# Low parts of weights later in VectorE's queue, two convolution blocks later, taps earlier

## The chip, the cores and the metric

The kernel runs on one core of one Trainium2 chip. The metric is device microseconds (us) of one execution, from launch to end; lower is better. A profiled execution also has a span, from its first to its last instruction.

## The reference

The reference is an encoder trunk of two layers with width 1024, applied with the same weights to a sequence of 256 tokens and to one of 512. It is all in float32. Per layer:

```
h  = rms_norm(x)                       # 768 tokens x 1024
q (8 heads), k, v (2 heads each), u (2 x 1024), gl (2 x 1024) = h @ w_in
q, k: rms_norm per head, rotary positions;  a = softmax(q k^T / sqrt(128)) v
c  = silu(layer_norm(conv31(u_a * sigmoid(u_g)))) @ w_pw     # depthwise, 31 taps
x += (sigmoid(gl_a) * a + sigmoid(gl_c) * c) @ w_out
x += (silu(gate) * up) @ w_down,  gate, up = rms_norm(x) @ w_gu   # 2816 wide
```

A last rms_norm follows the second layer. The change concerns what lies between `h` and `w_pw`: the projections, the attention and the convolution.

## The kernel before

**Layout and precision.** Activations lie with features on the 128 partitions and the 768 tokens along the free axis; a convolution chunk is 128 channels wide and there are 8 of them (j = 0 to 7). Each float32 operand is split into a high part (rounded by ScalarE) and a low part (the difference, by VectorE or GpSimd), and a product takes three matmuls: high by high, low by high, high by low. A weight block of 128 x 1024 arrives by DMA in a stage buffer (`Stage.load`, SP's queue); `Unit.make` has ScalarE write the high part and one other engine the low part. For all units of size 2 but those of `w_out` that engine is VectorE (`Weights.engines`, line 345). Stage buffers, high and low parts share a ring of 12 (N_W); at most four stage buffers are loaded ahead (`staged`, N_WS), and `Weights.pump` loads and splits the next block as soon as the counts let it.

**One program written by a planner.** The engines run their queues in program order, and the program order is written by a planner, `Clock`. Its `now` is advanced by each matmul at columns / 2400 us (`mm`, line 203), and its `dve` account by each VectorE instruction at elements / 960 us and a constant (`Vector`, line 133): 0.13 us, and TAP_MORE for a conv tap of 783 elements. A job given to `clock.at` or `clock.later` is written into the program once `now` has passed its due time, or before that when something calls it.

**The stream.** A layer's projections are blocks in the order of the list FILL: `ag2` (conv chunks 0 and 1, two weight blocks each), `k`, `q:0` to `q:3`, `v`, `gl:0` to `gl:15` (gates), `ag:2` to `ag:7` (a conv chunk each). The first seven run alone. Then attention begins: 48 units (8 heads x 6 query tiles) of scores, softmax, transposes and, for every two tiles, values; between their parts `fill` runs stream blocks for FILL_US planned us a unit. When FILL is done, the fill turns to the blocks of `w_pw` at the pace LATE_US.

**Softmax of a unit.** VectorE takes the row maximum (line 133, tile `h3t0st` for head 3, tile 0), ScalarE the exponential, GpSimd the reciprocal of the sum (line 1332), ScalarE scales, TensorE transposes (line 207), ScalarE and VectorE split the transposed tile.

**The convolution.** `ag_half` (line 795) takes a buffer for z, the gated input, out of three (N_Z). While three are live it issues taps, line 797: `while y.z_live >= N_Z: clock.tap()`. GpSimd then clears the padding of the new buffer (memset, line 803). A conv chunk is a first step on ScalarE and 30 taps on VectorE, each y += z shifted x weight (128 x 783). Two chunks are in progress at a time (`Clock.chains`) and their taps alternate. `Clock.tick` issues taps as long as `dve` is less than TAP_AHEAD = 1 us ahead of `now`. When all 8 chunks are summed, `channel_norm` runs LN_AFTER = 5.2 planned us later: means, centring, squares, variance, scaling, silu. The first pointwise block forces whatever of this has not been issued (`clock.force(y)`, line 895).

Of the kernel before, what the change touches and what calls it, by code (L numbers as in the profile page):

```python
# [118 lines left out]
class Vector:  # L119
# [5 lines left out]
    def __getattr__(self, name):  # L125
        f = getattr(self.engine, name)

        def call(out, *args, **kw):
            n = 1
            for d in (args[0].shape if name == "tensor_reduce" else out.shape)[1:]:  # L130
                n *= d
            self.clock.vector(n / 960.0 + (TAP_MORE if n == CONV_N else 0.13))
            return f(out, *args, **kw)  # L133
# [22 lines left out]
def trunk(tc, x_in, x_tok, w_a, w_qkv, w_pw, w_out, w_gu, w_down, vecs, gqk, rope, y_out):  # L156
    nc = tc.nc
    clock = Clock()
    vector = Vector(nc.vector, clock)

    with ExitStack() as ctx:
# [48 lines left out]
        def act(out, in_, func=AF.Copy, **kw):  # L210
            nc.scalar.activation(out, in_, func, **kw)  # L211

        def sub_lo(engine, lo, x, hi):
            engine.tensor_tensor(lo, x, hi.bitcast(F32), op=ALU.subtract)  # L214
# [6 lines left out]
        class Stage:  # L221


            def __init__(self, name, src):
                self.name, self.src, self.tile, self.last = name, src, None, None
# [5 lines left out]
        class Unit:  # L231
# [2 lines left out]

            def __init__(self, name, stages):
                self.name, self.stages, self.out, self.live = name, stages, None, False
                for stage in stages:
                    stage.last = self

            def make(self, engines):  # L240
                hi = wpool.tile([P, 1024], F32R, name="hi_" + self.name, tag="w", bufs=N_W)
                lo = wpool.tile([P, 1024], F32R, name="lo_" + self.name, tag="w", bufs=N_W)
                stage = self.stages[0].tile
                act(hi, stage)
                n = 1024 // len(engines)
                for i, e in enumerate(engines):
                    sl = slice(i * n, (i + 1) * n)
                    sub_lo(e, lo[:, sl], stage[:, sl], hi[:, sl])
                self.out = (hi, lo)

        class Quarter(Unit):

# [6 lines left out]
            def make(self, engines):  # L259
                src = self.quad.operand(self.m)  # L260
                both = wpool.tile([P, 1024], F32R, name="wq_" + self.name, tag="w", bufs=N_W)
                hi, lo = both[:, :512], both[:, 512:]
                act(hi, src)
                sub_lo(engines[0], lo, src, hi)
                self.out = (hi, lo)

        class Quad:

# [19 lines left out]
        class Weights:  # L288
# [36 lines left out]
            def split(self, engines=(nc.gpsimd,)):  # L325
                w = self.all[self.ready]
                while not self.here(w):
                    assert self.load()
                assert self.live + w.size + max(self.staged, N_WS) <= N_W
                self.live += w.size  # L330
                w.live = True
                w.make(engines)
                self.staged -= sum(stage.last is w for stage in w.stages)
                self.ready += 1
                self.next = max(self.next, clock.now + W_STEP[w.size - 1])

            def pump(self):
                while self.load():
                    pass
                if self.ready < len(self.all) and clock.now >= self.next:  # L340
                    w = self.all[self.ready]
                    if self.here(w) and self.live + w.size + max(self.staged, N_WS) <= N_W:
                        self.split(self.engines(w))
# [5 lines left out]
            def get(self, w):  # L349
                while w.out is None:  # L350
                    self.split(self.engines(self.all[self.ready]))
                return w.out

            def free(self, w):
# [60 lines left out]
        weights = Weights()  # L415
# [217 lines left out]
        def layer_blocks(l):  # L633
# [127 lines left out]
            def conv(j, z):  # L761
                wcol = lambda k: vcol(l, V_WDW, k * KC + j)

                def first():
                    y.y[j] = UC(nm(f"y{j}"))
                    act(y.y[j], z[:, :CONV_N], AF.Identity, scale=wcol(0), bias=vcol(l, V_BDW, j))
# [23 lines left out]
                def ready():  # L790
                    first()
                    clock.at(FIRST_AT[1], lambda: clock.waiting.append(taps))
                clock.at(FIRST_AT[0], ready)

# [45 lines left out]
            def gl_body(idx):  # L840
                def body(ws):
# [3 lines left out]
                    for s, (t0, n) in enumerate(SPLITS):  # L845
                        pg = yield from proj_a(ws[0], y.hT, s, nm(f"gl{idx}_{s}"))
                        act(sg[:, t0:t0 + n], pg[:, :n])
                        if s == 0 and FILL[-1] == f"gl:{idx}":
                            y.h_free = 1
# [9 lines left out]

            for b in FILL:  # L860
                kind, _, n = b.partition(":")
# [435 lines left out]
        def attention(y):  # L1297
# [7 lines left out]
            def scores(n):  # L1305
# [22 lines left out]

                late = stream.done((l, FILL[-1]))
                jobs[n] = [  # L1330
# [55 lines left out]
            def fill():  # L1386
                goal[0] += FILL_US / 2
                if not stream.done((l, FILL[-1])):
                    stream.run(goal[0], (l, FILL[-1]))
                    if stream.done((l, FILL[-1])):  # L1390
                        goal[0] = stream.work
                        goal[0] += PW_START
                        y.late = clock.now + 8.0
                        y.h_free = 2
                        split_z(y)
                elif y.m_done:
                    goal[0] = max(goal[0] + (LATE_US - FILL_US) / 2, stream.work)
                    stream.run(goal[0], (l, f"pw:{min(y.m_done, PW_MAX) - 1}"))
# [21 lines left out]
        def channel_norm(y):  # L1420
# [59 lines left out]
            def scale(j):  # L1480
                def f():
                    for s, (t0, n) in enumerate(SPLITS):
                        sl = slice(YO[s], YO[s] + n)
                        vector.tensor_tensor(ys[j][:, sl], ys[j][:, sl], rstd[s][:, :n], op=ALU.mult)
                    if j in SILU_AT:
                        clock.at(0.5, lambda: silus(j))
                return f

            def silus(j1):
                split_z(y)  # L1490
                for j in range(y.silus, j1 + 1):
                    act(ys[j], ys[j], AF.Silu, scale=vcol(l, V_LNG, j), bias=vcol(l, V_LNB, j))
                    y.silus += 1
                    split_z(y)
                if y.silus == KC:
                    y.normed()
# [116 lines left out]
        clock.drain()  # L1613


FILL = ["ag2", "k", "q:0", "gl:0", "ag:4", "ag:2", "ag:3", "gl:8", "v", "gl:9", "gl:1", "q:1", "ag:5", "ag:6",
        "gl:10", "gl:2", "q:2", "ag:7", "gl:3", "gl:14", "gl:12", "gl:4", "gl:11", "q:3", "gl:5", "gl:13", "gl:7",
        "gl:15", "gl:6"]
SILU_AT = (5, 7)
FIRST_AT = (1.2, 1.4)  # L1620
BURSTS = ((1, 7), (6, 4), (5, 2), (3,))
D_FIRST = (4.0, 6.0)
# [11 lines left out]
BEFORE = 7  # L1634
SIG_MAX = 3
SIG_LEFT = 25
FILL_US = 6.3
LATE_US = 3.7
PW_MAX = 10
PW_START = 3.0  # L1640
# [6 lines left out]
RSTD_AFTER = 5.4  # L1647
TABLES_AT = 16.0
TAP_AHEAD = 1.0
TAP_MORE = 0.13  # L1650
W_STEP = (0.9, 2.9)
A_EXP = 2.2
A_REC = (3.5, 2.5)
# [91 lines left out]
```

## Time and profile before

| | us |
|---|---|
| median of 3 runs | 2441.3 (2438.95 to 2444.44) |
| the profiled execution's own time | 2443.3 |
| its span | 2441.5 |
| TensorE busy in it | 2226.4 |
| VectorE busy in it | 1876.5 |

A row of a wait names the waiting engine, the tile and line it works on, and the instruction that released it. All operations of VectorE have line 133, most matmuls line 203, transposes line 207, and activations line 211, since helpers record them; so tiles are told by name: `L_y` a convolution's sum, `L_z` its input, `L_h3t0p` the probabilities of head 3, tile 0, `lo_L_wgl` the low part of a gate weight. In names `L0_` and `L1_` are both `L_`. Layer 0 runs from the start to about 1210 us, layer 1 after it; the same instruction appears some 1210 us later.

### The profile page before, as it was taken

How to read it: one execution, taken by the hardware profiler on the slowest of the kernel's cores; microseconds unless marked ns; L12 is line 12 of the kernel's file. 1: busy time of each engine (PE TensorE's matmuls, PEld its weight loads, DVE VectorE, ACT ScalarE, POOL GpSimd, SP SyncE). 2: the span in 40 equal slices, each digit the busy share in tenths (PEclk: the TensorE clock that was granted, in tenths of full speed). 3: DMA queues.
4: the chain of work that ended last, by engine and by line, in shares of the span. 5: the costliest groups of instructions: out<-in, count | busy, mean ns of one | idle time of the engine just before them, and what ended most of it. 6: DMA issues, size and time to landing. Idle time of an engine off the chain costs nothing. (4 is left out here: it accounts for less than half of the span.)

```text
span 2441.5 us, 34896 instructions
## 1 busy us (share of the span) xinstructions
PE 2226.4 (91%) x13276; PEld 2095.6 (86%) x13276; DVE 1876.5 (77%) x2484; ACT 1143.8 (47%) x2289; POOL 1068.2 (44%) x935
## 2 busy tenths in 40 slices
PE   8999869949979999999989998698699799999997
PEld 7989859848979999999988898596589799999997
DVE  5899768956387788798968897689553877987888
ACT  5446536555244444444443555465642444444443
POOL 3704132311256666666445142131112666666663
PEclk9999989969989999999999999899799899999998
DMA  4112111213312343343421111112142133333332
GB/s 165 61 57 69 66 39 63 77 43 113 133 49 90 121 144 116 124 145 113 152 85 61 63 63 57 50 63 72 54 146 101 35 121 127 124 130 137 122 123 87
DMA packets 72423, 229.59 MB, mean 94 GB/s; under 512 B 8128, under 2 KB 15296, under 8 KB 72256
## 3 DMA queue, kind: packets, MB, share of 16 engines
q1 hardware_dynamic: 72256, 227.37, 27.1%
q8 instruction: 104, 1.70, 0.3%
q14 instruction: 63, 0.52, 0.1%
HBM read 208.46 MB, written 18.87 MB: 93 GB/s over the span
## 5 line engine op out<-in xcount | busy, mean ns | idle before, releaser
L133 DVE SCALAR_TENSOR_TENSOR L_y<-L_z,vec,L_y 128x783 f32<-128x783 f32 x480 | 496.1, 1077 | 0.8
L214 POOL TENSOR_TENSOR wq_L_wgu_0m<-T_L_wgu,wq_L_wgu_0m 128x512 fp32r<-128x512 f32 x168 | 228.6, 1376 | 173.8 <-ACT wq_L_wgu_0m L211 173.8
L211 ACT ACTIVATE wq_L_wgu_0m<-T_L_wgu 128x512 fp32r<-128x512 f32 x168 | 102.7, 630 | 259.3 <-DVE T_L_wgu L133 208.7
L214 POOL TENSOR_TENSOR wq_L_wgu_0m<-st_L_wgu,wq_L_wgu_0m 128x512 fp32r<-128x512 f32 x126 | 179.3, 1425 | 43.4 <-ACT wq_L_wgu_0m L211 42.7
L203 PE MATMUL L_gl<-L_h1h,hi_L_wgl 128*128 128x512 f32 (+1 forms) x512 | 176.6, 345 | 0.0
L203 PE MATMUL L_gl<-L_h1h,lo_L_wgl 128*128 128x512 f32 (+1 forms) x512 | 173.2, 338 | 0.0
L203 PE MATMUL L_gl<-L_h1l,hi_L_wgl 128*128 128x512 f32 (+1 forms) x512 | 172.9, 338 | 0.0
L203 PEld LDWEIGHTS L_gl<-L_h1h,lo_L_wgl 128*128 128x128 f32 x512 | 97.0, 189 | 11.0
L203 PEld LDWEIGHTS L_gl<-L_h1l,hi_L_wgl 128*128 128x128 f32 x512 | 97.2, 190 | 9.2
L203 PEld LDWEIGHTS L_gl<-L_h1h,hi_L_wgl 128*128 128x128 f32 x512 | 97.0, 190 | 9.1
L203 PE MATMUL L_c<-L_zsl,hi_L_wpw 128*128 128x256 f32 (+1 forms) x256 | 89.2, 348 | 9.5 <-DVE L_zsl L133 9.5
L203 PE MATMUL L_c<-L_zsh,hi_L_wpw 128*128 128x256 f32 (+1 forms) x256 | 92.1, 360 | 4.6 <-ACT L_zsh L211 4.6
L203 PE MATMUL L_ug<-L_h1h,lo_L_wu 128*128 128x256 f32 (+1 forms) x256 | 89.0, 348 | 2.8 <-DVE lo_L_wu L133 2.8
L133 DVE TENSOR_TENSOR L_dl<-L_silu,L_dh 128x384 fp32r<-128x384 f32 x80 | 59.5, 783 | 41.0 <-ACT L_dh L211 41.0
L203 PE MATMUL L_ug<-L_h1h,hi_L_wu 128*128 128x256 f32 (+1 forms) x256 | 90.6, 354 | 0.0
L203 PE MATMUL L_ua<-L_h1h,lo_L_wu 128*128 128x256 f32 (+1 forms) x256 | 88.6, 346 | 1.4 <-DVE lo_L_wu L133 1.4
L203 PE MATMUL L_ua<-L_h1h,hi_L_wu 128*128 128x256 f32 (+1 forms) x256 | 89.7, 350 | 0.0
L203 PE MATMUL L_ug<-L_h1l,hi_L_wu 128*128 128x256 f32 (+1 forms) x256 | 89.5, 349 | 0.0
L211 ACT ACTIVATE wq_L_wgu_0m<-st_L_wgu 128x512 fp32r<-128x512 f32 x126 | 78.5, 623 | 22.8 <-POOL wq_L_wgu_0m L214 19.8
L203 PE MATMUL L_c<-L_zsh,lo_L_wpw 128*128 128x256 f32 (+1 forms) x256 | 88.9, 347 | 0.0
L203 PE MATMUL L_ua<-L_h1l,hi_L_wu 128*128 128x256 f32 (+1 forms) x256 | 88.1, 344 | 0.0
L203 PE MATMUL L_o<-L_mTlo,hi_L_wo 128*128 128x384 f32 x256 | 86.4, 338 | 0.0
(1630 smaller groups left out, 7626.7 us busy)
## 6 DMA issues: line engine op xcount, KB each, us to landing
st_L_wgu<-w_gu SPq DMA_DIRECT2D x88, 512.0 KB, 3.5
st_L_wu<-w_a SPq DMA_DIRECT2D x32, 512.0 KB, 3.5
st_L_wgl<-w_a SPq DMA_DIRECT2D x32, 512.0 KB, 3.5
st_L_wqkv<-w_qkv SPq DMA_DIRECT2D x24, 512.0 KB, 3.5
st_L_wpw<-w_pw SPq DMA_DIRECT2D x16, 512.0 KB, 3.5
st_L_wo<-w_out SPq DMA_DIRECT2D x16, 512.0 KB, 3.6
g_dram<-L_sgl SPq DMA_DIRECT2D x16, 384.0 KB, 3.0
L_gj<-g_dram SPq DMA_DIRECT2D x16, 384.0 KB, 3.8
```

What stands on the lines that cost most here:

```text
L133: return f(out, *args, **kw)
L203: nc.tensor.matmul(out, lhsT, rhs, start=start, stop=stop)
L211: nc.scalar.activation(out, in_, func, **kw)
L214: engine.tensor_tensor(lo, x, hi.bitcast(F32), op=ALU.subtract)
```

## The change

VectorE's low part of a weight block is no longer issued right after the high part but as a job due 1.6 planned us later (LO_AFTER), or when the block is first asked for by a matmul (`Weights.get`). The stage buffer counts as used once the low part is issued (`Weights.used`). In FILL, `ag:6` changes places with `gl:10`, and `ag:7` moves behind `gl:3` and `gl:14`. FILL_US goes from 6.3 to 6.5, and TAP_MORE from 0.13 to 0.02, so the planner books 0.11 us less for each conv tap. Instructions and their number stay the same.

```diff
--- before.py
+++ after.py
@@ -234,6 +234,7 @@
 
             def __init__(self, name, stages):
                 self.name, self.stages, self.out, self.live = name, stages, None, False
+                self.low = lambda: None
                 for stage in stages:
                     stage.last = self
 
@@ -243,10 +244,18 @@
                 stage = self.stages[0].tile
                 act(hi, stage)
                 n = 1024 // len(engines)
-                for i, e in enumerate(engines):
-                    sl = slice(i * n, (i + 1) * n)
-                    sub_lo(e, lo[:, sl], stage[:, sl], hi[:, sl])
+
+                def low():
+                    for i, e in enumerate(engines):
+                        sl = slice(i * n, (i + 1) * n)
+                        sub_lo(e, lo[:, sl], stage[:, sl], hi[:, sl])
+                    weights.used(self)
+
                 self.out = (hi, lo)
+                if engines == (vector,):
+                    self.low = clock.later(LO_AFTER, low)
+                else:
+                    low()
 
         class Quarter(Unit):
 
@@ -263,6 +272,7 @@
                 act(hi, src)
                 sub_lo(engines[0], lo, src, hi)
                 self.out = (hi, lo)
+                weights.used(self)
 
         class Quad:
 
@@ -330,9 +340,11 @@
                 self.live += w.size
                 w.live = True
                 w.make(engines)
-                self.staged -= sum(stage.last is w for stage in w.stages)
                 self.ready += 1
                 self.next = max(self.next, clock.now + W_STEP[w.size - 1])
+
+            def used(self, w):
+                self.staged -= sum(stage.last is w for stage in w.stages)
 
             def pump(self):
                 while self.load():
@@ -349,6 +361,7 @@
             def get(self, w):
                 while w.out is None:
                     self.split(self.engines(self.all[self.ready]))
+                w.low()
                 return w.out
 
             def free(self, w):
@@ -1613,10 +1626,11 @@
         clock.drain()
 
 
-FILL = ["ag2", "k", "q:0", "gl:0", "ag:4", "ag:2", "ag:3", "gl:8", "v", "gl:9", "gl:1", "q:1", "ag:5", "ag:6",
-        "gl:10", "gl:2", "q:2", "ag:7", "gl:3", "gl:14", "gl:12", "gl:4", "gl:11", "q:3", "gl:5", "gl:13", "gl:7",
+FILL = ["ag2", "k", "q:0", "gl:0", "ag:4", "ag:2", "ag:3", "gl:8", "v", "gl:9", "gl:1", "q:1", "ag:5",
+        "gl:10", "ag:6", "gl:2", "q:2", "gl:3", "gl:14", "ag:7", "gl:12", "gl:4", "gl:11", "q:3", "gl:5", "gl:13", "gl:7",
         "gl:15", "gl:6"]
 SILU_AT = (5, 7)
+LO_AFTER = 1.6
 FIRST_AT = (1.2, 1.4)
 BURSTS = ((1, 7), (6, 4), (5, 2), (3,))
 D_FIRST = (4.0, 6.0)
@@ -1634,7 +1648,7 @@
 BEFORE = 7
 SIG_MAX = 3
 SIG_LEFT = 25
-FILL_US = 6.3
+FILL_US = 6.5
 LATE_US = 3.7
 PW_MAX = 10
 PW_START = 3.0
@@ -1647,7 +1661,7 @@
 RSTD_AFTER = 5.4
 TABLES_AT = 16.0
 TAP_AHEAD = 1.0
-TAP_MORE = 0.13
+TAP_MORE = 0.02
 W_STEP = (0.9, 2.9)
 A_EXP = 2.2
 A_REC = (3.5, 2.5)
```

## Rows read from the trace of the kernel before

**Rows 1.** Page: span, and busy time of each engine.

```profile
span 2441.5 us, 34896 instructions
PE 2226.4 (91%) x13276; PEld 2095.6 (86%) x13276; DVE 1876.5 (77%) x2484; ACT 1143.8 (47%) x2289; POOL 1068.2 (44%) x935
```

**Rows 2.** Waits of TensorE: waiter, releaser: us in total, times, longest.

```profile
PE L_h3t0T L207 <- ACT L_h3t0p L211: 42.6, 2, 21.3
PE L_var L203 <- DVE L_sq L133: 40.3, 2, 20.1
...
PE L_h1t5T L207 <- ACT L_h1t5p L211: 13.0, 2, 6.5
...
PE L_rstd L207 <- DVE L_rb L133: 5.2, 2, 2.6
PE L_c L203 <- ACT L_zsh L211: 4.6, 2, 2.3
```

**Rows 3.** Timeline of VectorE: start, us, instruction, count.

```profile
247.66 8.59 DVE L133 SCALAR_TENSOR_TENSOR L_y<-L_z,vec,L_y 128x783 f32<-128x783 f32 x9
...
324.03 15.20 DVE L133 SCALAR_TENSOR_TENSOR L_y<-L_z,vec,L_y 128x783 f32<-128x783 f32 x16
```

**Rows 4.** Timeline of GpSimd; in brackets idle time before and its releaser.

```profile
256.31 0.20 POOL L803 MEMSET L_z<- 128x15 f32 x3 [12.74 <-DVE L_y L133]
...
339.29 0.20 POOL L803 MEMSET L_z<- 128x15 f32 x3 [19.29 <-DVE L_y L133]
...
344.59 0.54 POOL L1332 TENSOR_TENSOR L_h3t0st<-L_h3t0st,nones 128x1 f32<-128x1 f32 x1
```

**Rows 5.** Windows: length, busy PE, PEld, DVE, ACT, POOL, clock, DMA.

```profile
339.50:376.00 36.50, 30.28 (x164) 26.24 (x165) 15.90 (x24) 20.00 (x38) 7.01 (x9) 0.86 0.25 83
376.00:483.40 107.40, 107.40 (x692) 97.04 (x691) 97.74 (x120) 62.44 (x134) 33.85 (x33) 1.00 0.21 72
240.00:483.40 243.40, 215.58 (x1372) 194.20 (x1371) 194.60 (x241) 130.20 (x274) 62.42 (x71) 0.94 0.18 61
1450.00:1693.40 243.40, 215.57 (x1367) 194.30 (x1367) 193.49 (x240) 130.44 (x275) 62.39 (x71) 0.94 0.18 61
```

**Rows 6.** Timeline of VectorE and TensorE at the end of the convolution.

```profile
483.41 0.96 DVE L133 TENSOR_TENSOR L_ysum<-L_ysum,L_y 128x783 f32<-128x783 f32 x1
484.43 1.56 PE L203 MATMUL L_mean<-L_ysum,ones 128*128 128x256 f32 x4 [0.18 <-DVE L_ysum L133]
...
515.24 0.58 PE L203 MATMUL L_c<-L_zsh,hi_L_wpw 128*128 128x256 f32 x1 [2.30 <-ACT L_zsh L211]
```

**Rows 7.** Timeline of TensorE: first score matmuls, three units apart.

```profile
402.66 0.39 PE L203 MATMUL L_h4t2s<-L_kThi,L_q2Thi 128*128 128x512 f32 x1
...
429.44 0.39 PE L203 MATMUL L_h4t5s<-L_kThi,L_q2Thi 128*128 128x512 f32 x1
```

**Rows 8.** Window of instructions on L_z: length, DVE, ACT, POOL, clock, DMA.

```profile
376.00:483.40 107.40, 66.73 (x66) 1.03 (x1) 0.00 (x0) 1.00 0.21 72
```

**Rows 9.** Group of VectorE, 50 to 240 us: busy, mean ns, idle before.

```profile
L133 DVE SCALAR_TENSOR_TENSOR L_y<-L_z,vec,L_y 128x783 f32<-128x783 f32 x114 | 119.9, 1095 | 0.2
```

**Rows 10.** Windows after the two waits, columns as in rows 5.

```profile
264.30:268.00 3.70, 3.70 (x11) 3.12 (x12) 1.12 (x3) 2.43 (x6) 0.54 (x1) 0.51 0.11 35
345.60:350.00 4.40, 4.28 (x12) 3.48 (x13) 2.16 (x3) 3.17 (x9) 0.10 (x1) 0.52 0.20 62
```

**Rows 11.** Groups of VectorE, 240 to 484 us, columns as in rows 9.

```profile
L133 DVE SCALAR_TENSOR_TENSOR L_y<-L_z,vec,L_y 128x783 f32<-128x783 f32 x125 | 127.1, 1059 | 0.2
L133 DVE TENSOR_TENSOR lo_L_wgl<-st_L_wgl,hi_L_wgl 128x1024 fp32r<-128x1024 f32 x12 | 15.4, 1281 | 19.1 <-ACT hi_L_wgl L211 19.1
L133 DVE TENSOR_TENSOR lo_L_wqkv<-st_L_wqkv,hi_L_wqkv 128x1024 fp32r<-128x1024 f32 x4 | 4.9, 1223 | 4.1 <-ACT hi_L_wqkv L211 4.1
```

**Rows 12.** Timeline of TensorE: the wait for a weight's low part.

```profile
101.71 0.39 PE L203 MATMUL L_ua<-L_h1h,lo_L_wu 128*128 128x256 f32 x1 [0.57 <-DVE lo_L_wu L133]
```

**Rows 13.** Timeline of GpSimd: a reciprocal beside taps.

```profile
281.52 1.31 POOL L1332 TENSOR_TENSOR L_h2t2st<-L_h2t2st,nones 128x1 f32<-128x1 f32 x1 [9.05 <-ACT L_h2t2p L211]
```

## The prediction

> **What bounds the kernel now.** I read five views in this order.
>
> The page's busy line first [rows 1]: TensorE is busy for 2226.4 of 2441.5 us. So 215 us is the most that any reordering can win unless it removes work, and this change removes none. The question is which of these 215 us hang on what is moved.
>
> Second, what TensorE waited for [rows 2]. Two waits lead, each occurring once in each of the two layers: 21.3 us ahead of the transposes of head 3, tile 0, and 20.1 us ahead of the variance matmul. A third, 6.5 us, stands ahead of the transposes of h1t5. All lie between the projections and the first pointwise matmul of a layer, where the change is.
>
> Third, VectorE and GpSimd at the two transposes [rows 3, 4]. VectorE runs 9 and then 16 conv taps in an unbroken row. GpSimd's memset of a new z buffer waits 12.74 and 19.29 us for just these taps. That is line 797: ag:6 and ag:7 start with three z buffers live, and the planner issues taps until one comes free. The maximum of a score tile, the rotary products and the softmax reciprocal stand behind them, so the transposes wait.
>
> Fourth, the stretch by windows [rows 5]: from 240 to 483.4 us TensorE needs 215.58 us of 243.4, VectorE 194.60, so VectorE idles 48.8 us. Layer 1 gives the same (215.57, 193.49). Of the idle time 36.5 − 15.90 = 20.6 us follow the 16 taps: they raised the planner's VectorE account by 15 us, so for that long it offers no tap while the engine stands empty.
>
> Fifth, the end of the stretch [rows 6]: the means start at 484.43, the first pointwise matmul at 515.24. In between TensorE waits 20.1 + 2.6 + 2.3 = 25.0 us [rows 2] for the layer norm. The conv's last tap sets that norm's start, and VectorE sets the last tap.
>
> **The change part by part.** First the planner's scale, since two edits are in planned us. A three-step run of score tiles takes 429.44 − 402.66 = 26.78 us, 8.93 us a unit [rows 7]. The code plans such a unit at 6.3 (FILL_US) + 0.64 (scores) + 0.64 (half a values step) + 0.44 (four turns) = 8.02. One planned us is 1.11 us.
>
> *Order.* ag:6 comes one gate block later, ag:7 two. A gate block is 24 × (256 + 512) / 2400 = 7.68 planned us of stream work, and a unit grants 6.5 of it in 8.22, so the delays are 9.7 and 19.4 planned us. How many taps pass meanwhile? From 376 to 483.4 us, where TensorE never idles [rows 5], 66 taps ran [rows 8]. The planner books 0.946 us for one (783/960 + 0.13), together 62.4 of 107.4 / 1.11 = 96.6 planned us, so 34.2 go to other VectorE work: 0.35 per us. At the new 0.836 a planned us holds 0.646 / 0.836 = 0.77 taps: 7.5 pass ahead of ag:6 and 15 ahead of ag:7, where 9 and 16 are forced today. The taps put in sooner cover the rest: of the 114 between 50 and 240 us [rows 9] each is booked 0.11 shorter, 15 more taps by then if all were paced, some 7 as part are forced. Both runs should vanish. Removed per layer: 6.5 + 21.3 us of waiting. After them TensorE runs at 0.51 and 0.52 of its clock (the lower level, 1.2 GHz) for 3.7 and 4.4 us [rows 10], costing 1.8 + 2.1 us. Together 31.7 us. The moved weights' loads move with them on SP's queue; their number is unchanged, and the DMA share here is 0.18 [rows 5].
>
> *Taps sooner.* In a paced stretch the planner is full, so its booking sets VectorE's rate. With 0.836 the 376 to 483.4 stretch holds (96.6 − 34.2) / 0.836 = 74.6 taps, 8.6 more. A tap takes 15.20 / 16 = 0.95 us back to back [rows 3], so VectorE needs 97.74 + 8.2 = 105.9 of 107.4 us, 99%. That is full, not over. What the faster pace costs if it doesn't fit is a rival below.
>
> *Low parts later.* VectorE now stands still for low parts whose high part ScalarE hasn't made: 19.1 + 4.1 us in this stretch, 16 instructions [rows 11]. Issued 1.6 planned us later, taps ahead of them fill that time; without this the 99% would not be had. Nothing is added. The stage buffer is counted free 1.6 us later, which delays a load by as much; a gate weight's four-deep lead hides it. Where the lead is missing it costs: at 101.71 TensorE already waits 0.57 us for a low part [rows 12]. There a deferred one can come 1.8 us later, or two taps (1.9 us). At one or two such places, bounds 0 and 4 us a layer; I take 2, since only one wait of this kind shows.
>
> *FILL_US.* The stream after the first seven blocks holds 15 × 7.68 + 7 × 15.36 = 222.7 planned us: 35.3 units at 6.3, 34.3 at 6.5. One attention unit, 1.72 planned or 1.9 us, moves behind the fill and is done there. I take nothing, bounds −2 to +2 us a layer.
>
> *What is late next: the norm.* Without the two waits TensorE reaches the end of the fill at 484.4 − 31.7 − 1.9 = 451. When is the last tap? 125 taps and all else took VectorE 194.6 us [rows 5, 11]. Some 7 taps fall ahead of 240 (−6.7), and the attention work behind the new end is left out (about −6): 182 us, at 97% 188, so the last tap falls near 428 instead of 483. The norm is due 6.7 planned us later, about 436, and has 15 us under the fill; paced, not forced, it does perhaps 10 us' worth of its 31 there. The 25.0 us become 15. Gain 10 a layer, bounds 0 (all of it reappears) and 25 (all hidden).
>
> Sum: 2 × (31.7 − 2 + 10) = 79 us. From the profiled execution's 2443.3 us that gives 2364; the median shown is 2 us lower, 2441.3, so I forecast 2362.
>
> One rule speaks against denser taps. A reciprocal on GpSimd takes 0.54 us when VectorE rests and 1.31 us beside taps [rows 4, 13]. The Trainium skill, "SBUF — State Buffer", section "Who interferes with whom", says a VectorE instruction with two SBUF inputs contends with a GpSimd instruction that reads SBUF; a tap has two. The two rows agree. By that rule every one of the 34 units a layer could pay 0.77 us, at most 52 us over both layers if none were hidden, and the sum would be 27 us; by the rows most reciprocals are slow already and none but the 21 us one shows up as a TensorE wait, so I leave the sum.
>
> **The rivals.**
>
> *The wait passes to the variance.* For: VectorE, not TensorE, decides the conv's end, and forced taps were work it had to do anyway. Then only the 20.6 us of idle time behind the 16 taps is won per layer: 41 us, 2400. Against: the low-part waits go as well.
>
> *Taps are still forced at ag:7's new place.* If half of that stall stays and the norm gains nothing: 2 × (8.3 + 11.7) = 40 us, 2401. Against: the count above has 6 taps to spare.
>
> *The norm hides wholly.* 2 × (31.7 − 2 + 25) = 109 us, 2332. For: the last tap would come 23 us ahead of the fill's end. Against: the norm waits between its steps are planned in us, so unforced it is longer than 31.
>
> *Slower: VectorE is oversubscribed.* At 99% any stretched tap makes it fall behind the plan; then each unit's maximum and low part of the probabilities stand behind one or two taps more, and TensorE waits at each transpose. At 1.5 us for each of 34 units in two layers that is 102 us, less 63 for the stalls: 2480. It decides from 63 / 68 = 0.9 us a unit. For: taps of 1.06 us mean [rows 11] against 0.836 booked. Against: the maximum today shows up in no wait of TensorE outside the forced runs, and a wait stops the planner's clock too, so the lag doesn't grow.
>
> *It does nothing.* The conv's end stays, every us won reappears at the variance: 2441. Against: this needs new VectorE idle time of 50 us.
>
> **How the numbers follow.** Forecast 52%, with its own range of 2342 (norm gain 20) to 2382 (none). Wait passes on 16%, forced at the new place 8%, norm hidden 12%, slower 8%, nothing 4%. Between 2336 and 2410 lie the forecast, the two at 2400 and a small part of the hidden norm, 8 in 10. A measurement of this kernel tells about 0.2%, 5 us, from no change: faster 0.52 + 0.16 + 0.08 + 0.12 = 0.88, same 0.04, slower 0.08.
>
> **What would show it.** Right if: the memsets for the sixth and seventh z wait under 2 us, no run of taps longer than about 6 outside the first 150 us, no wait of 5 us at the h3t0 and h1t5 transposes, VectorE's waits for high parts of weights under 8 us in the stretch, its busy share there over 93%, and the variance wait near 10 us. Wrong in the pace if many small TensorE waits for probabilities appear; wrong in the norm if the variance wait stays at 20 us or grows; wrong altogether if a run of taps stands in front of a memset at another place.

## The result, and the profile of the changed kernel

The changed kernel takes 2348.34 us (median, 2345.87 to 2351.65) against 2442.55 before: a ratio of 0.9617, 95% interval 0.9598 to 0.9636, or 94 us less. The forecast was 2362. The profiled execution took 2350.5 us.

Page of the changed kernel: span, and busy time of each engine.

```profile
span 2348.7 us, 34918 instructions
...
PE 2215.4 (94%) x13276; PEld 2089.7 (89%) x13276; DVE 1880.5 (80%) x2484; ACT 1157.4 (49%) x2299; POOL 1079.0 (46%) x935
```

TensorE and VectorE have as many instructions as before; TensorE's busy time falls by 11.0 us, VectorE's grows by 4.0 [rows 1]. The rest of the 92.8 us that the span lost is idle time of TensorE.

Waits of TensorE in the changed kernel (total, times, longest), to be laid beside [rows 2]:

```profile
PE L_c L203 <- ACT L_zsh L211: 11.6, 2, 5.8
PE L_c L203 <- DVE L_zsl L133: 9.3, 2, 4.6
...
PE L_h4t4T L207 <- ACT L_h4t4p L211: 6.3, 2, 3.5
PE L_h1t2T L207 <- ACT L_h1t2p L211: 6.0, 2, 3.0
...
PE L_v L203 <- DVE lo_L_wqkv L133: 4.4, 2, 2.2
PE L_q0T L207 <- DVE L_kTlo L133: 4.4, 2, 2.2
...
PE L_h0t0T L207 <- ACT L_h0t0p L211: 3.9, 2, 2.0
```

The waits of 21.3 us at h3t0, 20.1 at the variance and 6.5 at h1t5 are gone, in both layers. In their place stand small ones of 2 to 3.5 us, where the kernel before had none or at most 1.3, and 5.8 us ahead of the first pointwise matmul, where it had 2.3. The wait for `L_zsl` is no new one: it was 9.5 us in both layers before.

GpSimd's memsets for the sixth, seventh and eighth z buffer (the two of [rows 4] are the seventh and eighth):

```profile
234.22 0.20 POOL L816 MEMSET L_z<- 128x15 f32 x3
...
267.60 0.20 POOL L816 MEMSET L_z<- 128x15 f32 x3
...
334.76 0.20 POOL L816 MEMSET L_z<- 128x15 f32 x3
```

No bracket: none waits for a tap, where two had waited 12.74 and 19.29 us.

Groups of VectorE from 240 us to the convolution's end in the changed kernel, answering to [rows 11]:

```profile
L133 DVE SCALAR_TENSOR_TENSOR L_y<-L_z,vec,L_y 128x783 f32<-128x783 f32 x118 | 120.8, 1059 | 0.5
L133 DVE TENSOR_TENSOR lo_L_wgl<-st_L_wgl,hi_L_wgl 128x1024 fp32r<-128x1024 f32 x11 | 13.9, 1268 | 3.2 <-ACT hi_L_wgl L211 3.1
L133 DVE TENSOR_TENSOR lo_L_wqkv<-st_L_wqkv,hi_L_wqkv 128x1024 fp32r<-128x1024 f32 x4 | 4.9, 1220 | 0.8 <-ACT hi_L_wqkv L211 0.7
```

For the high parts of these weights VectorE waits 3.1 + 0.7 = 3.8 us instead of 23.2. The windows show what that makes of the stretch (columns as in [rows 5]): up to the end of the convolution, the norm under the fill, and the pointwise stage.

```profile
240.00:436.90 196.90, 190.35 (x1228) 171.89 (x1227) 182.63 (x229) 121.90 (x256) 71.27 (x70) 0.99 0.21 67
...
434.00:476.00 42.00, 36.20 (x218) 31.54 (x216) 28.58 (x49) 31.27 (x53) 4.22 (x7) 0.99 0.26 87
476.00:574.00 98.00, 93.36 (x563) 83.01 (x564) 57.73 (x87) 61.06 (x109) 24.78 (x24) 0.95 0.32 109
```

VectorE is busy for 182.63 of 196.9 us, 93%, against 194.60 of 243.4, 80%. In the second window TensorE works 36.20 of 42 us while the norm runs; before, the 30.8 us from the means to the first pointwise matmul held 25.0 us of waits [rows 2, 6].

The end of the convolution, beside [rows 6]:

```profile
431.76 0.97 DVE L133 TENSOR_TENSOR L_ysum<-L_ysum,L_y 128x783 f32<-128x783 f32 x1
434.15 1.46 PE L203 MATMUL L_mean<-L_ysum,ones 128*128 128x256 f32 x4
...
461.56 1.40 PE L203 MATMUL L_var<-ones,L_sq 128*128 128x2 f32 x12
...
475.89 0.58 PE L203 MATMUL L_c<-L_zsh,hi_L_wpw 128*128 128x256 f32 x1 [5.80 <-ACT L_zsh L211]
```

The last sum comes at 431.76 instead of 483.41, the means 50.3 us sooner, the first pointwise matmul 39.3 us sooner. From means to pointwise the norm takes 41.7 us now that most of it is paced by the planner; forced, it took 30.8. But TensorE has gate blocks and attention to run meanwhile.

### The profile page after: what moved, and what is told of

Read it like the earlier page. It is cut to its first block, busy times and chain, and to the rows that moved or that the text cites. A ratio compares the mean times of both kernels' runs of the same rounds, so it can differ in the third digit from the quotient of the medians.

```text
span 2348.7 us, 34918 instructions
## 1 busy us (share of the span) xinstructions
PE 2215.4 (94%) x13276; PEld 2089.7 (89%) x13276; DVE 1880.5 (80%) x2484; ACT 1157.4 (49%) x2299; POOL 1079.0 (46%) x935
## 5 line engine op out<-in xcount | busy, mean ns | idle before, releaser
L203 PE MATMUL L_c<-L_zsh,hi_L_wpw 128*128 128x256 f32 (+1 forms) x256 | 91.5, 357 | 11.6 <-ACT L_zsh L211 11.6
```

The lines of the kernel that those rows point to most:

```text
L203: nc.tensor.matmul(out, lhsT, rhs, start=start, stop=stop)
```

## The experiments

Each run is compared with the kernel before on the same chip. The last three columns are of layer 0: "means" is when the means start, "forced" the wait of the memsets for the seventh and eighth z, "variance" TensorE's wait ahead of the variance matmul, all in us.

| run | us | ratio, 95% interval | means | forced | variance |
|---|---|---|---|---|---|
| before | 2443 | 1 | 484.4 | 12.7, 19.3 | 20.1 |
| order alone | 2396.0 | 0.9809 (0.9792 to 0.9825) | 460.1 | 9.3, 7.8 | 18.7 |
| pace alone | 2378.5 | 0.9734 (0.9719 to 0.9748) | 438.0 | 7.1, 0 | none |
| deferral alone | 2426.1 | 0.9926 (0.9912 to 0.9941) | 477.7 | 11.6, 17.3 | 19.4 |
| all but the order | 2345.6 | 0.9597 (0.9583 to 0.9612) | 432.5 | 4.7, 0 | none |
| all but the pace | 2378.0 | 0.9733 (0.9718 to 0.9747) | 458.2 | 5.3, 9.1 | 19.2 |
| all but the deferral | 2397.0 | 0.9806 (0.9791 to 0.9821) | 441.6 | 0, 0 | 2.3 |
| all but FILL_US | 2343.8 | 0.9594 (0.9581 to 0.9607) | 434.5 | 2.5, 0 | none |
| pace and order | 2374.0 | 0.9718 (0.9705 to 0.9731) | 441.3 | 1.3, 0 | none |
| pace and deferral | 2342.2 | 0.9587 (0.9573 to 0.9600) | 430.7 | 6.9, 0 | none |
| changed, again | 2350.4 | 0.9620 (0.9606 to 0.9633) | 430.3 | 0, 0 | none |

### Each part alone, and the order taken away

The three parts are edits of the kernel before; the fourth run is the changed kernel with the old list.

```diff
order alone:     -FILL = [... "ag:5", "ag:6", "gl:10", ... "q:2", "ag:7", "gl:3", "gl:14", "gl:12", ...]
                 +FILL = [... "ag:5", "gl:10", "ag:6", ... "q:2", "gl:3", "gl:14", "ag:7", "gl:12", ...]
pace alone:      -TAP_MORE = 0.13
                 +TAP_MORE = 0.02
deferral alone:  + low(), Weights.used, LO_AFTER = 1.6 of the change
no order:        the changed kernel with the old FILL
```

> The kernel before with the new block order alone (ag:6 one gate block later, ag:7 two). Theory A (the order takes the forced taps away, the pace and the later low parts let the convolution end earlier): the 6.5 and 21.3 us waits fall under 3 us each and the memsets of the sixth and seventh z wait under 4 us, but VectorE keeps its old pace, so the variance wait stays at 20 us or grows towards 28; 2385 to 2405 us. Theory B (the pace frees the z buffers, the order adds little): the forced runs stay above half of their 9 and 16 taps; 2425 to 2440. Theory C (VectorE alone decides, so the wait only passes to the variance): both waits go, the variance wait grows by about as much; 2400 to 2440.

Order alone, TensorE's longest wait in the stretch and a memset ahead of ag:7:

```profile
PE L_var L203 <- DVE L_sq L133: 37.3, 2, 18.7
```

```profile
339.69 0.20 POOL L803 MEMSET L_z<- 128x15 f32 x3 [7.75 <-DVE L_y L133]
```

2396 us. The forced waiting falls by 3.4 and 11.5 us, and that is enough: the wait at h3t0 is 2.0 us, and none shows at h1t5. The memsets still wait 9.3 and 7.8 us where theory A had said under 4. The variance wait stays. By the time and by TensorE's waits theory A holds for the order alone: the two waits go, and little else.

> The kernel before with TAP_MORE 0.02 alone. Theory A: the run of 16 forced taps shrinks to 2 to 8 and that of 9 to 0 to 3, so of the 27.8 us of waits some 15 go, and the convolution ends 10 us earlier relative to the fill; 2390 to 2415 us. Theory B: both forced runs vanish and the norm hides, 2350 to 2375. Theory C: 2415 to 2440, with a longer variance wait. If a VectorE that is offered more taps only falls behind, many small waits of TensorE for probabilities appear and the time is above 2445.

```profile
238.75 0.19 POOL L803 MEMSET L_z<- 128x15 f32 x3
262.08 0.20 POOL L803 MEMSET L_z<- 128x15 f32 x3 [7.06 <-DVE L_y L133]
...
325.33 0.19 POOL L803 MEMSET L_z<- 128x15 f32 x3
```

2378.5 us, between theories A and B. The pace alone takes the run of 16 taps away wholly and shortens that of 9, and starts the means 46 us sooner, so the variance wait goes too. VectorE is busy for 182.26 of the 198.0 us from 240 us to the means, 92%, with no low part deferred. Small waits appear: 5.3 us at h0t0, 4.1 at h3t0, 2.7 at h4t5.

> The kernel before with the low parts of weights deferred alone. Theory A: VectorE's waits for high parts of weights fall from 23 us to under 8 us between 240 and 484 us, but the planner offers no more taps than before, so the idle time reappears elsewhere; 2430 to 2445 us. Theory C: the same. If idle time of VectorE at low parts was what made the convolution late, 2400 to 2425.

2426.1 us. Group of VectorE from 240 to 480 us in this run:

```profile
L133 DVE TENSOR_TENSOR lo_L_wgl<-st_L_wgl,hi_L_wgl 128x1024 fp32r<-128x1024 f32 x12 | 14.9, 1242 | 5.4 <-ACT hi_L_wgl L211 5.4
L133 DVE TENSOR_TENSOR lo_L_wqkv<-st_L_wqkv,hi_L_wqkv 128x1024 fp32r<-128x1024 f32 x4 | 4.9, 1221 | 0.9 <-ACT hi_L_wqkv L211 0.8
```

23.2 us of VectorE's waiting become 6.2, and the kernel gains 18 us over two layers; both forced runs and the variance wait stay. That is 4 us more than either theory gave: the idle time does not all reappear.

> The changed kernel with the old block order. Theory A: the forced run ahead of ag:7 is back at about half its length, a wait of 8 to 14 us per layer at a transpose near 320 us; 2370 to 2395 us. Theory B: no forced run, 2345 to 2358. Theory C: the wait at the transposes is back and the variance wait is shorter for it; 2348 to 2365.

2345.6 us: theory B. Without the new order the memset of the eighth z waits for nothing, that of the seventh 4.7 us without a wait of TensorE behind it:

```profile
233.86 0.19 POOL L816 MEMSET L_z<- 128x15 f32 x3
260.70 0.20 POOL L816 MEMSET L_z<- 128x15 f32 x3 [4.72 <-DVE L_y L133]
...
321.41 0.19 POOL L816 MEMSET L_z<- 128x15 f32 x3
```

So theory A falls in its first half. The order can take the two waits away, but beside the pace it has nothing left to take.

### The pace and the deferral taken away

```diff
no pace:      -TAP_MORE = 0.02
              +TAP_MORE = 0.13
no deferral:  -                if engines == (vector,):
              +                if False:
```

> The changed kernel with TAP_MORE back at 0.13 (order, deferral and FILL_US stay). Theory A (order and pace do the same thing to the forced taps, and only the pace ends the convolution early): no wait over 4 us at a transpose, but the variance wait is back at 12 to 20 us a layer, since the means start 15 to 25 us later than the 434 of the changed kernel; 2372 to 2395 us. Theory B2 (the order and the deferral suffice, the pace is spare): variance wait under 6 us, 2345 to 2360.

2378.0 us, theory A. The longest wait at a transpose is 5.4 us, at h1t2, over the 4 that theory A allowed; none stands behind the two forced memsets. But the variance wait is back at full length, since the means start at 458:

```profile
PE L_var L203 <- DVE L_sq L133: 38.4, 2, 19.2
...
PE L_h1t2T L207 <- ACT L_h1t2p L211: 10.8, 2, 5.4
```

Order and deferral do not end the convolution early; in all profiles the means start between 430 and 442 us with the faster pace and between 458 and 484 without.

> The changed kernel with the low parts issued at once (order, pace and FILL_US stay). Theory A: VectorE's waits for high parts of weights are back at 15 to 25 us between 240 and 440 us, its busy share there falls from 93% to 85 to 88%, it lags the planner, and small waits of TensorE at transposes or at the means take up 10 to 15 us a layer; 2365 to 2380 us. Theory B2 (the deferral is spare once taps are dense): 2345 to 2355.

2397.0 us, above both theories: without the deferral the changed kernel loses 47 to 49 us (2350.4 and 2348.3 with it, on other chips), and is slower than with the pace alone. VectorE waits 14 us for high parts from 240 to 440 us, and is busy for 182.84 of the 201.6 us up to the means, 91%; theory A had 15 to 25 us and 85 to 88%:

```profile
DVE lo_L_wgl L133 <- ACT hi_L_wgl L211: 7.3, 3, 5.5
DVE lo_L_wqkv L133 <- ACT hi_L_wqkv L211: 3.7, 2, 2.0
DVE lo_L_wu L133 <- ACT hi_L_wu L211: 3.0, 1, 3.0
```

The norm wait of TensorE is short (2.3 us at the variance), so the loss lies elsewhere. In layer 0 the kernel is 4.7 us later than the changed one when h1t0 starts, 8 us at h2t0 and h3t0, 12 at h5t0, 15 at the first pointwise matmul and 25 at the output projection. Windows from 50 us to the output projection, first of the changed kernel, then of this run:

```profile
50.00:573.80 523.80, 499.27 (x3235) 453.15 (x3234) 442.35 (x566) 301.28 (x631) 174.96 (x179) 0.98 0.22 74
50.00:598.40 548.40, 509.36 (x3236) 459.10 (x3235) 441.55 (x566) 298.90 (x631) 162.99 (x179) 0.97 0.22 72
```

Of the 24.6 us, 14.5 are idle time of TensorE (39.0 against 24.5), in waits of at most 5 us; in the other 10.1 it runs the same matmuls more slowly, at a granted clock of 0.97 against 0.98.

### FILL_US, and pairs of parts

```diff
no FILL_US:          the changed kernel, -FILL_US = 6.5
                                         +FILL_US = 6.3
pace and order:      the kernel before with the new FILL and TAP_MORE = 0.02
pace and deferral:   the changed kernel with the old FILL and FILL_US = 6.3
```

> The changed kernel with FILL_US back at 6.3. If FILL_US only moves one attention unit behind the fill, the time is within 5 us of the changed kernel, 2343 to 2353 us. If the wider grant is what gives the softmax its room between units (VectorE has 3% more time a unit), transposes wait more and it is 2355 to 2370.

2343.8 us, in the range expected of an attention unit that only changes its place, though 6.6 us below the changed kernel on this chip. The wait of 3.0 us at h1t2 is gone, and one of 4.9 us stands at h3t0 instead.

> The kernel before with pace and order, low parts at once, FILL_US 6.3. The pace alone gave 2378.5 and pace, order and FILL_US 2397. If the order is what costs without the deferral (the two conv blocks' weights then fall where ScalarE is late with high parts), 2392 to 2402; if FILL_US does, 2374 to 2384, as the pace alone.

2374.0 us: it is FILL_US that costs some 23 us where nothing is deferred, not the order. Up to the means both runs take 441 us. Two windows of each, from the means to the pointwise stage and through it, show half of layer 0's loss in each. First all but the deferral, then pace and order:

```profile
441.00:491.00 50.00, 43.31 (x249) 37.34 (x247) 30.46 (x51) 33.62 (x58) 4.75 (x8) 0.97 0.18 61
491.00:598.00 107.00, 96.32 (x560) 84.53 (x561) 58.07 (x90) 61.69 (x111) 22.74 (x24) 0.94 0.35 115
```

```profile
441.00:484.00 43.00, 38.29 (x226) 33.20 (x225) 28.68 (x49) 30.64 (x51) 4.23 (x7) 0.98 0.21 70
484.00:584.50 100.50, 92.22 (x555) 81.16 (x556) 57.55 (x87) 59.00 (x106) 23.43 (x23) 0.96 0.33 111
```

With FILL_US at 6.5 TensorE has 23 matmuls or 5.0 us more to do between means and pointwise, and stands still for 6.7 us instead of 4.7; in the pointwise stage it is busy 4.1 us longer, at a clock of 0.94 against 0.96, and stands still for 10.7 us instead of 8.3. That it stands one attention unit further back fits. Why the same costs so little once the low parts are deferred, no run isolates.

> The kernel before with pace and deferral alone; order and FILL_US as before. If the parts simply add (65 and 18 us) 2358 to 2364. If pace and deferral help each other, since the taps fill what a low part would wait for, 2342 to 2352, as without the order; then neither the order nor FILL_US is needed.

2342.2 us, below the sum of the parts. Pace and deferral gain 65 and 18 us alone and 101 together: the deferral is worth 36 us beside the pace. From pace alone this run differs by the deferral only. It starts the output projection of layer 0 at 570.5 us instead of 586.5, and 13.6 of these 16.0 us are waits of TensorE: among them h0t0's fall from 5.3 to 2.0, and 2.7 at h4t5, 2.2 at a conv chunk's first matmuls and 1.9 at h1t5 are gone. TensorE's waits in this run:

```profile
PE L_c L203 <- ACT L_zsh L211: 9.8, 2, 4.9
PE L_c L203 <- DVE L_zsl L133: 9.3, 2, 4.7
PE L_h3t0T L207 <- ACT L_h3t0p L211: 8.2, 2, 4.2
```

> The changed kernel itself, beside the three on the same chip: 2345 to 2352 us. It is the measure for the order: if it is 1 to 4 us above the changed kernel with the old order (2345.6), the order costs a little here rather than gains.

2350.4 us on the same chip as the three runs before it. The interval of pace and deferral alone (0.9573 to 0.9600) lies below that of the changed kernel (0.9606 to 0.9633): the two-part version beats both kernels, by 101 and 8 us in the median. Where the 8 us lie is not shown: one of the five executions of the changed kernel, the profiled one, took 2341.8 us, as long as the two-part version. With FILL_US at 6.3 the order makes no difference (0.9594 with it, 0.9587 without).

### Two attempts to win more

```diff
norm sooner, on the old order:   -VAR_AFTER = 4.0        +VAR_AFTER = 2.5
                                 -RSTD_AFTER = 5.4       +RSTD_AFTER = 4.4
pace late, on the old order:     TAP_MORE is 0.13 until a layer's attention starts, 0.02 from there
```

> The changed kernel with the old block order and two steps of the channel norm planned sooner (VAR_AFTER 4.0 to 2.5, RSTD_AFTER 5.4 to 4.4), to win from both kernels. If the wait of 5.8 us ahead of the first pointwise matmul is the norm's planned pace, it falls by 1 to 3 us a layer and the time is 2339 to 2344 us; if it is ScalarE's silu and VectorE's scaling, which are issued when the pointwise block forces them, 2344 to 2348, and a wait at the variance of 1 to 2 us may appear.

2344.1 us, ratio 0.9590 (0.9574 to 0.9606), no different from the 0.9597 without the edit. The wait ahead of the pointwise matmul falls from 5.8 to 4.9 us and the next from 4.6 to 2.5, but h6t0's transposes now wait 2.0. The rest is scaling, silu and splitting, which the pointwise block forces.

> The changed kernel with the old block order and the faster pace only from the start of the attention (0.13 before it in each layer). If the pace before the attention costs the waits of TensorE between 100 and 245 us (some 10 us a layer at the low parts, the k transposes and h0t0 and h1t2), these fall below 5 us and the convolution ends up to 8 us later; 2335 to 2345 us. If those waits come from VectorE being full whatever the pace there, 2344 to 2352; if the earlier taps are what lets the norm hide, 2352 to 2365 with a norm wait that is longer by 5 to 10 us.

2353.1 us, ratio 0.9629 (0.9614 to 0.9643), 7 to 8 us slower than with the faster pace throughout (2345.6). The early waits do shrink: those at v's low part and at h0t0 are gone. But the means start at 438.5, and the norm shows again. TensorE's waits in this run (one helper line more, so lines are one higher):

```profile
PE L_c L204 <- DVE L_zsl L134: 9.5, 2, 4.7
PE L_h5t5T L208 <- ACT L_h5t5p L212: 8.5, 2, 4.7
PE L_h1t2T L208 <- ACT L_h1t2p L212: 7.8, 2, 4.0
...
PE L_rstd L208 <- DVE L_rb L134: 6.5, 2, 3.8
```

In layer 0 the first pointwise matmul comes 4.0 us sooner than with the faster pace throughout (470.3 against 474.3), yet the output projection 2.7 us later (577.2 against 574.5): the pointwise stage takes 106.9 us instead of 100.3, with 4.7 us of waiting at h5t5 and a granted clock of 0.92 instead of 0.95. So the small waits before the attention buy taps that pay later. The time is that of the third case, but the waits of the norm are only 2.4 us longer, not 5 to 10.

## Why the prediction was right, and where it was not

The time lies in the forecast's own range, 14 us below it. By its steps, per layer:

| step | forecast | measured |
|---|---|---|
| the two waits (27.8) and the slow clock behind them (3.9, reckoned from [rows 10]) | 31.7 | 31.7, none is left |
| new small waits | −2 | −11.8 |
| norm wait (25.0 us before) | 10 | 19.2 (5.8 left) |
| pointwise stage | 0 | 8.9 |
| sum | 39.7 | 48.0 |

The output projection starts 48.2 us sooner in layer 0 (573.8 against 622.0), which checks the sum. The windows from 50 us check it another way. That of the kernel before, to be laid beside the changed kernel's under "The pace and the deferral taken away":

```profile
50.00:622.00 572.00, 504.70 (x3236) 455.26 (x3235) 443.07 (x569) 294.94 (x628) 165.78 (x179) 0.94 0.21 70
```

TensorE stands still for 24.5 us instead of 67.3, and as many matmuls take 5.4 us less, at a granted clock of 0.98 instead of 0.94. That the sum comes within 14 us is in part luck: two terms are 9 to 10 us a layer off each, in opposite directions, and a stage that was not forecast gives the rest.

**The forced runs** went as said, but not for the reason that carried the count. I let the order pass 7.5 and 15 taps and gave the pace "some 7". Alone, the order took 3.4 and 11.5 us off the forced waits, and the pace 5.7 and 19.3. (The 7.5 and 15 are at the new pace; at the old one the same reckoning gives 6.6 and 13.) The step that failed is "some 7 as part are forced": the pace gives all that the eighth z needs. With both, the order is spare.

**The pace.** The last tap was forecast near 428 us, and the last sum came at 431.8. VectorE's share was to be 97 to 99%, with over 93% as the sign, and is 92.8%; the rival in which it falls behind and makes the kernel slower did not come. Its mechanism is there in small: 0.6 + 2.2 + 0.9 + 1.5 + 3.0 + 3.5 us more at a low part, v, the k transposes, h0t0, h1t2 and h4t4, 11.8 us where I had 2. Those at v and h0t0 are the pace's: they stand in the run with the pace alone (2.0 and 5.3 us) and are absent, or 0.5 us at most, from every run in which the early pace is the old one. They stand behind one more run of taps, just past the 150 us up to which the prediction allowed such runs:

```profile
150.62 11.79 DVE L133 SCALAR_TENSOR_TENSOR L_y<-L_z,vec,L_y 128x783 f32<-128x783 f32 x11
...
163.27 0.42 DVE L133 TENSOR_REDUCE L_h0t0st<-L_h0t0s 128x1 f32<-128x256 f32 x1
...
164.54 1.22 DVE L133 TENSOR_TENSOR lo_L_wqkv<-st_L_wqkv,hi_L_wqkv 128x1024 fp32r<-128x1024 f32 x1
```

Every run with the faster pace before the attention has a row of 11 or 12 taps that begins between 148 and 154 us; no run with the old early pace has one. The wait at h1t2 is not the pace's: it stands, at 3.0 to 5.4 us, in every run with FILL_US at 6.5, the one without the pace among them, and in none with 6.3.

**The deferral.** I gave it no gain of its own and said that without it the 99% would not be had. That reason does not hold: without it VectorE's share up to the means is 91 to 92% in the three runs with the faster pace, against 92.8% with it, and the means start at 438.0 to 441.6 us. The deferral is worth 18 us alone, 36 beside the pace and 47 to 49 in the changed kernel, and beside the pace most of that is small waits of TensorE. The loss of 2 us a layer that I put down to late low parts does not show in the run with the deferral alone; in the changed kernel it is the 0.6 us above. The interplay with FILL_US stays open.

**The norm** is the term that was mis-sized: 19.2 us won where I had 10. I took the end of the fill at 451 us and 15 us of cover. It is 469, the last gate matmuls before the pointwise block: 11.8 of the 18 us are the small waits, and the rest I estimate at 5 us of slower clock (0.98 and 0.99 up to the means) and the norm's own matmuls, which now run inside the fill. The means started at 434.2 instead of 436, only 2.4 us behind the last sum. So the norm had 35 us of cover. The two errors offset each other: a TensorE held up by small waits meets a norm that is further on.

**The pointwise stage** was not forecast. From the first pointwise matmul to the output projection it took 106.8 us and takes 97.9. The waits at h6t0, h6t4 and h7t4 (5.7, 0.4 and 1.1 us) are gone; that is 7.2 of 8.9 us, although one attention unit more (h5t5) runs there. Why they went is not shown. The forced norm ahead of them is not reason enough: in the run without the pace the norm is forced as well, no wait stands at h6t0, and the stage takes 101.1 us.

**The reciprocals beside taps.** Denser taps were to lengthen GpSimd's reciprocals by at most 52 us in all. The 96 reciprocals took 81.7 us before and take 90.7, and GpSimd's busy time grew from 1068.2 to 1079.0 us: a fifth of that bound. The trace agrees in direction with the rule of the Trainium skill, "SBUF — State Buffer", section "Who interferes with whom", that the prediction cites. How much of it reaches TensorE is not shown.

## What to carry to other kernels

Where a program is written ahead by a model of its engines, look at how the model books the engine that others wait for. Here 0.11 us more for each of 480 taps left VectorE idle for a fifth of the stretch, where the pace alone leaves 8%, made the planner force taps in runs, and put a layer norm in the open. Correct the booking first. Moving blocks around treated the places where the error showed, and added nothing once it was corrected. Deferring an instruction that stands still for another engine's result was worth 18 us alone and twice that together with work that fills the gap.

## What the runs showed that I had not expected

What an edit is worth depends on its company: the order gains 48 us alone and nothing beside the pace and the deferral, the deferral 18 us alone and 47 to 49 in the changed kernel, and FILL_US costs 3 to 7 us with the deferral and some 23 without. And the norm's chain takes 41.7 us instead of 30.8 when it shares its engines with attention, yet 5.8 us of it are seen instead of 25.0.
